# A hybrid encoder layer on one core: B parts moved behind the first block, the last pair's work laid out anew, one bank seeded

## The chip, the cores and the metric

The kernel runs on one core of a Trainium2 chip. The metric is the device time of one execution in microseconds (us). TensorE is called PE here, VectorE DVE, ScalarE ACT, GpSimd POOL and SyncE SP.

## The reference, cut to what matters

One layer is computed for 256 prompt rows and 128 sample rows (8 streams of 16), 384 rows in all, in float32, model width 2048.

```
u = rmsnorm(x);  proj = u @ w_in            # pool | z | xBC | dt | gates
A: pooling over windows 2, 4, 8, 16, a linear map per group
B: xbc = silu(causal_conv(xBC));  x, Bm, Cm = split(xbc)
   decay = exp(cum_t - cum_s) where s <= t
   y = (Cm Bm^T * decay) @ (x * dt) + (Cm @ h) * exp(cum)
   h = h * exp(last) + Bm^T (w_end * x * dt)
   y = gated_rmsnorm(y + d_skip * x, z)
m = sigmoid(g_A) * (A @ w_pool_proj) + sigmoid(g_B) * (y @ w_ssd_proj)
x = x + rmsnorm(m @ w_out)
x = x + rmsnorm(relu(rmsnorm(x) @ w_up)^2 @ w_down)
```

The outputs are the two parts of x and the new pooling, convolution and scan states.

## The kernel before, in words

Activations lie transposed in SBUF (features on the partitions, 384 rows in the free dimension). Every product with float32 weights is made of three matmuls: weight and activation are each cut into a high and a low part, and high*high, high*low and low*high are summed in one PSUM bank. For this each weight tile of 128x1024 (512 KB) is loaded by SP, cast by ACT into its high part (`wh`, line 70), and DVE subtracts to get the low part (`wl`, line 71). The three kinds of tile (`w`, `wh`, `wl`) have three buffers each, so the cast of a tile waits until PE is through with the tile three before it. A projection of 128 columns takes two such tiles, here called its halves; each is 24 matmuls (lines 101 to 103).

The scan stage runs over 8 groups of 8 heads. A group projects and convolves six column blocks (x in four, B and C), then z in four. Every group has two pairs of four heads. The work of a pair on ACT and DVE is in small functions:

- `xside`: x, turned by way of a DRAM buffer, times dt (`xdt`) and times the state's weights (`xT`), then cut into high and low (`xhl`)
- `eside(S, q)`: eight pieces of the exponent's argument (`E`) for two heads; with q = 1 the Exp over all four follows
- `dside`: the state (`hs`) times its decay; `fside(S, h2)`: half of `E` times the masked product of C and B (`cbm`)
- `bside`: B, turned, cut into high and low (`Bhl`), and two masked copies (`Bm`)

The products of a pair on PE stand in a block between two projections: `t_pp` (`pp`), `t_cb` (`cb`), `t_yT` and `t_Y` (`Y`), `t_yi` (`py`), `state` (`su`). The work of a group's second pair is spread over the next group's projections. Behind the last group there is no next one, so the last pair's work is spread over the projections of the second gate: `gate_b` calls `between` behind each half, and this takes the next piece from a list.

Every engine runs its instructions in order, and this order is decided when the program is built. `behind(ins)` puts instructions behind `ins` in that order, and `later()` puts them behind the last cast and the last subtraction of weights.

The down projection adds eight parts of 1024 features. For each part and each of four blocks of 512 columns, PE fills three PSUM banks (`wd`, one for each 128 rows `b`), and `done(b)` adds a bank to the sum in SBUF (`hacc`, line 1336). In the last part the sum is squared on ACT with the row sums in `st3` (line 1340); the last block's sum times the norm's weights goes to `z3` (line 1347); `postnorm` takes the root; line 1351 makes the four blocks of the output rows and SP stores them. In the last block all four weight tiles are held, and PE does the rows `b` = 0, 1, 2 one after the other.

## Time and profile before

| | |
|---|---|
| median of 3 runs | 2649.3 us (2647.81 to 2649.31) |
| profiled execution | 2648.75 us |
| its span, first to last instruction | 2647.0 us |
| PE busy | 2632.5 us (99%) |
| DVE busy | 1545.5 us (58%) |
| ACT busy | 1161.5 us (44%) |
| mean granted clock of TensorE | 0.999 |

A row of the timeline has the start in the span, the busy time, the engine, the line, the operation, the tiles and the count; in brackets stand the engine's idle time before it and what ended that. A row of the chain has start, length and what ran.

### The profile page before, as it was taken

To read this page: it belongs to the slowest core of one execution; us is meant where nothing else is said; L and a number is where in the kernel's file an instruction comes from. 1 tells how busy PE (TensorE), PEld (TensorE's weight loads), DVE (VectorE), ACT (ScalarE), POOL (GpSimd) and SP (SyncE) were. 2 spreads that over 40 slices of the span, in tenths; PEclk is the share of its full clock that TensorE was granted. 3 is DMA by queue.
4 is the path that set the end of the run, shared out by engine and by line. 5 is a ranking of instruction groups with operands and counts; after the bars stand their busy time and mean duration, and the time that the engine had idled before them with its cause. 6 is when DMAs were issued, how large, how long until landed. Compare 5 with 4: busy or idle time off the path is not lost.

```text
span 2647.0 us, 40715 instructions
## 1 busy us (share of the span) xinstructions
PE 2632.5 (99%) x16317; PEld 2528.3 (96%) x16317; DVE 1545.5 (58%) x2192; ACT 1161.5 (44%) x1780; POOL 242.5 (9%) x382
## 2 busy tenths in 40 slices
PE   9999999999999999999999999999999999999998
PEld 9999999999999999999999989999999999989897
DVE  6685334788888888867444436534444444444446
ACT  6443323657565656545333335433333333323233
POOL 0000002123222322311000000000000000000000
PEclk9999999999999999999999999999999999999999
DMA  7444446566666666657555543444444344444443
GB/s 275 149 133 159 148 145 207 193 200 226 215 235 197 218 228 227 221 184 257 168 162 162 188 155 134 142 137 134 137 135 137 133 137 134 136 135 137 135 137 130
DMA packets 130175, 451.50 MB, mean 171 GB/s; under 512 B 17921, under 2 KB 24641, under 8 KB 124993
## 3 DMA queue, kind: packets, MB, share of 16 engines
q1 hardware_dynamic: 103552, 361.57, 41.8%
q0 software_dynamic: 19520, 72.64, 7.7%
q10 hardware_dynamic: 6912, 14.68, 1.8%
q8 instruction: 128, 2.10, 0.3%
q14 instruction: 63, 0.51, 0.1%
HBM read 404.49 MB, written 44.34 MB: 170 GB/s over the span
## 4 chain that ended last, share of the span: by engine, by line
PE 96%; DVE 1%; DMA 1%; ACT 1%; issue 0%; POOL 0%; SPq 0%; DVEq 0%; POOLq 0%; ACTq 0%
PE pj_up L102 6%; PE pj_up L103 6%; PE pj_up L101 6%; PE wd L156 6%; PE wd L154 6%; PE wd L155 6%; PE pj_x L101 4%; PE pj_x L102 4%; PE pj_x L103 4%; PE pj_z L103 3%; PE pj_z L102 3%; PE pj_sp L102 3%; PE pj_sp L101 3%; PE pj_sp L103 3%; PE pj_z L101 3%; PE pj_ga L101 2%
## 5 line engine op out<-in xcount | busy, mean ns | idle before, releaser
L101 PE MATMUL pj_up<-x1h,wh_up 128*128 128x384 f32 (+1 forms) x1024 | 333.7, 326 | 0.0
L102 PE MATMUL pj_up<-x1l,wh_up 128*128 128x384 f32 (+1 forms) x1024 | 333.4, 326 | 0.0
L103 PE MATMUL pj_up<-x1h,wl_up 128*128 128x384 f32 (+1 forms) x1024 | 333.4, 326 | 0.0
L71 DVE TENSOR_TENSOR wl_wd<-w_wd,wh_wd 128x1024 fp32r<-128x1024 f32 x126 | 154.3, 1225 | 240.5 <-ACT wh_wd L70 240.5
L154 PE MATMUL wd<-wh_wd,hh 128*128 128x512 f32 x756 | 286.5, 379 | 0.0
L155 PE MATMUL wd<-wl_wd,hh 128*128 128x512 f32 x756 | 286.5, 379 | 0.0
L156 PE MATMUL wd<-wh_wd,hl 128*128 128x512 f32 x756 | 286.5, 379 | 0.0
L70 ACT ACTIVATE wh_wd<-w_wd 128x1024 fp32r<-128x1024 f32 x126 | 133.1, 1057 | 322.3 <-PE wd L156 261.8
L70 ACT ACTIVATE wh_up<-w_up 128x1024 fp32r<-128x1024 f32 x126 | 133.1, 1057 | 292.0 <-PE pj_up L102 231.8
L71 DVE TENSOR_TENSOR wl_up<-w_up,wh_up 128x1024 fp32r<-128x1024 f32 x126 | 154.3, 1224 | 178.1 <-ACT wh_up L70 178.0
L101 PE MATMUL pj_x<-xgh,wh_x 128*128 128x384 f32 x768 | 252.1, 328 | 0.0
L103 PE MATMUL pj_x<-xgh,wl_x 128*128 128x384 f32 x768 | 250.5, 326 | 0.1
L102 PE MATMUL pj_x<-xgl,wh_x 128*128 128x384 f32 x768 | 250.4, 326 | 0.0
L102 PEld LDWEIGHTS pj_up<-x1l,wh_up 128*128 128x128 f32 x1024 | 193.6, 189 | 0.2
L101 PEld LDWEIGHTS pj_up<-x1h,wh_up 128*128 128x128 f32 x1024 | 193.6, 189 | 0.2
L103 PEld LDWEIGHTS pj_up<-x1h,wl_up 128*128 128x128 f32 x1024 | 193.6, 189 | 0.0
L103 PE MATMUL pj_z<-xgh,wl_z 128*128 128x384 f32 x512 | 167.3, 327 | 0.0
L101 PE MATMUL pj_z<-xgh,wh_z 128*128 128x384 f32 x512 | 166.9, 326 | 0.0
L102 PE MATMUL pj_z<-xgl,wh_z 128*128 128x384 f32 x512 | 166.9, 326 | 0.0
L101 PE MATMUL pj_sp<-abh,wh_sp 128*128 128x384 f32 x512 | 166.9, 326 | 0.0
L102 PE MATMUL pj_sp<-abl,wh_sp 128*128 128x384 f32 x512 | 166.9, 326 | 0.0
L103 PE MATMUL pj_sp<-abh,wl_sp 128*128 128x384 f32 x512 | 166.9, 326 | 0.0
(330 smaller groups left out, 6180.9 us busy)
## 6 DMA issues: line engine op xcount, KB each, us to landing
w_up<-w_up SPq DMA_DIRECT2D x128, 512.0 KB, 3.5
w_wd<-w_down SPq DMA_DIRECT2D x128, 512.0 KB, 3.5
w_x<-w_in SPq DMA_DIRECT2D x96, 512.0 KB, 4.1
w_z<-w_in SPq DMA_DIRECT2D x64, 512.0 KB, 4.2
w_sp<-w_ssd SPq DMA_DIRECT2D x64, 512.0 KB, 3.5
w_ga<-w_ga SPq DMA_DIRECT2D x32, 512.0 KB, 3.5
w_pp<-w_pp SPq DMA_DIRECT2D x32, 512.0 KB, 3.5
hs<-ssm POOLq DMA_DIRECT2D x16, 1024.0 KB, 7.5
```

The costliest lines, as they stand in the source:

```text
L70: cut[0] = s.activation(h, w, AF.Copy)
L71: cut[1] = v.tensor_tensor(l, w, h.bitcast(F32), ALU.subtract)
L101: te.matmul(out, wh, xh, start=first, stop=False, **how)
L102: te.matmul(out, wh, xl, start=False, stop=False, **how)
L103: return te.matmul(out, wl, xh, start=False, stop=last, **how)
L154: te.matmul(out, mh, vh, start=k == 0, stop=False)
L155: te.matmul(out, mh, vl, start=False, stop=False)
L156: last[0] = te.matmul(out, ml, vh, start=False, stop=k == nk - 1)
```

## The change

Three places change.

First, `xside` and `eside` are cut in two (`hside` has the cut of x, `expside` the Exp), which leaves the order in the groups as it is, and in the first group `bside` is put behind the cut of the first pair's x.

```diff
             cload(D.p[1])
-            bside(D)
+            with nullcontext() if g else behind(S.split):
+                bside(D)
             dside(S)
```

On ACT in the first group stood this before (`xs1` is a block of x, `xs40` the convolved C, `wh_x3_0` the cast of a weight half):

```order
L615 ACTIVATE xs1_4391<-cacc1_4386,vec_71 128x384
L70 ACTIVATE wh_x2_1_4429<-w_x2_1_4427 128x1024
L723 ACTIVATE Bhl0_4745<-Bt0_4304 128x384
L70 ACTIVATE wh_x3_0_4476<-w_x3_0_4474 128x1024
L600 COPY cbuf0_4137<-cbuf0_4137 128x15x3
L601 COPY cstate_4135<-cbuf0_4137 128x27
L609 ACTIVATE cacc40_4464<-cbuf0_4137,vec_71 128x384
L599 COPY cbuf0_4137<-cstate_4135 128x8x3
L615 ACTIVATE xs40_4469<-cacc40_4464,vec_71 128x384
```

Now the third of these rows is gone from there, and later in the same group, on ACT, it stands here:

```order
L609 ACTIVATE cacc3_4645<-cbuf2_4141,vec_71 128x384
L779 ACTIVATE E0_0_4652<-cbc0_0_1_4307,tok_629 128x128
L723 ACTIVATE Bhl0_4745<-Bt0_4304 128x384
L788 ACT_TABLE_LOAD
L788 ACTIVATE E0_0_4652<-E0_0_4652 128x2048
L615 ACT_TABLE_LOAD
L615 ACTIVATE xs3_4650<-cacc3_4645,vec_71 128x384
```

Only this instruction moved on ACT in that group; DVE's row, POOL's and SP's are the same.

Second, the last pair's work has eight places instead of six, one behind each half of the four gates.

```diff
                 work = [
-                    lambda: xside(S),
-                    lambda: eside(S, 0),
-                    lambda: eside(S, 1),
-                    lambda: dside(S),
-                    lambda: fside(S, 0),
-                    lambda: fside(S, 1),
+                    [lambda: xside(S)],
+                    [lambda: hside(S), lambda: eside(S, 0)],
+                    [],
+                    [lambda: eside(S, 1)],
+                    [lambda: dside(S)],
+                    [lambda: expside(S)],
+                    [lambda: fside(S, 0), lambda: fside(S, 1)],
+                    [],
                 ]
```

On ACT before, from the cut of the last pair's x (`xhl7_1`) to its Exp (`wh_gb2_0` is the first half of the third gate, so the fifth half; `gbt` is a gate's sigmoid):

```order
L768 ACTIVATE xhl7_1_12254<-xT7_1_11723 128x768
L70 ACTIVATE wh_gb1_1_12259<-w_gb1_1_12257 128x1024
L777 ACTIVATE E7_1_12287<-cbc7_1_0_11888,tok_629 128x128 x8
L70 ACTIVATE wh_gb2_0_12303<-w_gb2_0_12301 128x1024
L570 ACT_TABLE_LOAD
L570 ACTIVATE gbt0_12296<-gbt0_12296 128x384
L777 ACTIVATE E7_1_12287<-cbc7_1_1_11890,tok_629 128x128 x8
L70 ACTIVATE wh_gb2_1_12342<-w_gb2_1_12340 128x1024
L785 ACT_TABLE_LOAD
L785 ACTIVATE E7_1_12287<-E7_1_12287 128x2048
L70 ACTIVATE wh_gb3_0_12378<-w_gb3_0_12376 128x1024
```

And now, over the same stretch of ACT:

```order
L70 ACTIVATE wh_gb1_1_12256<-w_gb1_1_12254 128x1024
L770 ACTIVATE xhl7_1_12284<-xT7_1_11723 128x768
L779 ACTIVATE E7_1_12287<-cbc7_1_0_11888,tok_629 128x128 x8
L70 ACTIVATE wh_gb2_0_12303<-w_gb2_0_12301 128x1024
L570 ACT_TABLE_LOAD
L570 ACTIVATE gbt0_12296<-gbt0_12296 128x384
L70 ACTIVATE wh_gb2_1_12333<-w_gb2_1_12331 128x1024
L779 ACTIVATE E7_1_12287<-cbc7_1_1_11890,tok_629 128x128 x8
L70 ACTIVATE wh_gb3_0_12376<-w_gb3_0_12374 128x1024
L570 ACTIVATE gbt1_12369<-gbt1_12369 128x384
L70 ACTIVATE wh_gb3_1_12407<-w_gb3_1_12405 128x1024
L788 ACT_TABLE_LOAD
```

The fourth half's cast (`wh_gb1_1`) moved ahead of the cut of x, the sixth's (`wh_gb2_1`) ahead of the second eight pieces of E, and the Exp moved from behind the sixth half's cast to behind the eighth's (`wh_gb3_1`). DVE's row follows: its half of the fourth weight half ahead of `xhl`, `hs` behind the seventh, and both products of E behind the ninth.

Third, in the last part and block of the down projection, bank 2 is filled with the sum so far before PE starts on it; its matmuls add to that, and `done(2)` uses the bank itself as the sum. The last product and the last store of the output are cut into two halves of 256 columns, and ACT issues the second store.

```diff
+                end = c8 == NC - 1 and nb == 3
+                held = 2 if end else None
+                if end:
+                    s.copy(o[held], hacc[:, held, blk(nb)])
...
-                    v.tensor_tensor(dst, o[b], dst, ALU.add)
+                    if b == held:
+                        dst = o[b]
+                    else:
+                        v.tensor_tensor(dst, o[b], dst, ALU.add)
...
-                        sy.dma_start(io["y"][b][:, blk(i)], z)
+                        for n, c in enumerate((slice(0, 256), slice(256, 512)) if b + i == 5 else (slice(0, 512),)):
...
+                            (s if n else sy).dma_start(io["y"][b][:, blk(i)][:, c], z[:, c])
```

In `moving`, the matmuls of the held bank have no `start`:

```diff
-            te.matmul(out, mh, vh, start=k == 0, stop=False)
+            te.matmul(out, mh, vh, start=k == 0 and b != held, stop=False, skip_group_check=b == held)
```

On DVE the end of the program was this (`wd7_3_2` is the bank, `n3_n32` the root):

```order
L1336 TENSOR_TENSOR hacc_17042<-wd7_3_2_24472,hacc_17042 128x512
L1347 TENSOR_TENSOR z3_2_24623<-hacc_17042,gpo2_17043 128x512
L1037 TENSOR_SCALAR n1_n32_24626<-st3_17046,n0_n32_24625 128x1
L1038 RECIPROCAL n3_n32_24628<-n2_n32_24627 128x1
L1039 TENSOR_SCALAR n1_n32_24626<-n1_n32_24626,n3_n32_24628 128x1
L1041 SCALAR_TENSOR_TENSOR n3_n32_24628<-n1_n32_24626,n3_n32_24628 128x1
L1351 SCALAR_TENSOR_TENSOR hacc_17042<-hacc_17042,n3_n32_24628,x1_15707 128x512 x3
L1351 SCALAR_TENSOR_TENSOR z3_2_24623<-z3_2_24623,n3_n32_24628,x1_15707 128x512
```

Now it is:

```order
L1364 TENSOR_TENSOR z3_2_24623<-wd7_3_2_24472,gpo2_17043 128x512
L1047 TENSOR_SCALAR n1_n32_24626<-st3_17046,n0_n32_24625 128x1
L1048 RECIPROCAL n3_n32_24628<-n2_n32_24627 128x1
L1049 TENSOR_SCALAR n1_n32_24626<-n1_n32_24626,n3_n32_24628 128x1
L1051 SCALAR_TENSOR_TENSOR n3_n32_24628<-n1_n32_24626,n3_n32_24628 128x1
L1369 SCALAR_TENSOR_TENSOR hacc_17042<-hacc_17042,n3_n32_24628,x1_15707 128x512 x3
L1369 SCALAR_TENSOR_TENSOR z3_2_24623<-z3_2_24623,n3_n32_24628,x1_15707 128x256 x2
```

The add is gone, `z3` reads the bank and waits for ACT's square of the same bank, and the last product stands twice at half the size. On ACT the copy into the bank stands behind the squares of the second block, and the square of the last rows (now line 1357) reads the bank.

More of the change, by code (lines that the diff above doesn't have):

```diff
@@ L143, in proj, with moving @@
         return o
-    def moving(o, units, lhs, tail, done, pool=None, own=0, hook=None, mid=None):
+    def moving(o, units, lhs, tail, done, pool=None, own=0, hook=None, mid=None, held=None):
         nk = 2 * len(units)
@@ L153, in mm @@
             out, vh, vl = pairs(o[b]), woven(wh[:, c]), woven(wl[:, c])
-            te.matmul(out, mh, vh, start=k == 0, stop=False)
-            te.matmul(out, mh, vl, start=False, stop=False)
-            last[0] = te.matmul(out, ml, vh, start=False, stop=k == nk - 1)
+            te.matmul(out, mh, vh, start=k == 0 and b != held, stop=False, skip_group_check=b == held)
+            te.matmul(out, mh, vl, start=False, stop=False, skip_group_check=b == held)
+            last[0] = te.matmul(out, ml, vh, start=False, stop=k == nk - 1, skip_group_check=b == held)
         for kp in range(n - tail):
@@ L766, in xside, with hside @@
                     )
+        def hside(S):
             S.xhl = pd.tile([P, 2, 2, 3, P], F32R, tag="xhl", name=f"xhl{S.nm}", bufs=1)
@@ L783, in eside, with expside @@
                     )
-            if q:
-                s.activation(S.E, S.E, AF.Exp, scale=-1.0)
+        def expside(S):
+            s.activation(S.E, S.E, AF.Exp, scale=-1.0)
         def fside(S, h2):
@@ L874, in build @@
                 work = [
-                    lambda: xside(S),
-                    lambda: eside(S, 0),
-                    lambda: eside(S, 1),
-                    lambda: dside(S),
-                    lambda: fside(S, 0),
-                    lambda: fside(S, 1),
+                    [lambda: xside(S)],
[6 more added lines that the diff above has]
+                    [],
                 ]
                 def between():
-                    if work:
-                        with later():
-                            work.pop(0)()
+                    with later():
+                        for fn in work.pop(0):
+                            fn()
                 for i in range(4):
@@ L907, in build @@
                 xside(prev.p[1])
+                hside(prev.p[1])
             xturned(D, g, 0)
@@ L915, in build @@
                 eside(prev.p[1], 1)
+                expside(prev.p[1])
             cload(D.p[0])
@@ L945, in build @@
                 xside(S)
+                hside(S)
             xturned(D, g, 2)
@@ L962, in build @@
                 eside(S, 1)
+                expside(S)
             cload(D.p[1])
-            bside(D)
+            with nullcontext() if g else behind(S.split):
+                bside(D)
             dside(S)
@@ L1350, in done @@
                         z = z3 if i == 3 else hacc[:, b, blk(i)]
-                        v.scalar_tensor_tensor(
-                            out=z, in0=z, scalar=y, in1=x1[:, b, blk(i)], op0=ALU.mult, op1=ALU.add
-                        )
-                        sy.dma_start(io["y"][b][:, blk(i)], z)
+                        for n, c in enumerate((slice(0, 256), slice(256, 512)) if b + i == 5 else (slice(0, 512),)):
+                            v.scalar_tensor_tensor(
+                                out=z[:, c], in0=z[:, c], scalar=y, in1=x1[:, b, blk(i)][:, c], op0=ALU.mult, op1=ALU.add
+                            )
+                            (s if n else sy).dma_start(io["y"][b][:, blk(i)][:, c], z[:, c])
                 moving(
@@ L1359, in build @@
                     hh,
-                    4 if c8 == NC - 1 and nb == 3 else 0,
+                    4 if end else 0,
                     done,
                     pg,
-                    2 if c8 == NC - 1 and nb == 3 else 0,
+                    2 if end else 0,
+                    held=held,
                 )
```

## The prediction

> **What bounds the kernel now.** I read the page first, then the waits of TensorE (PE), then the chain of work that ended last, in three stretches.

> ```profile
> span 2647.0 us, 40715 instructions
> PE 2632.5 (99%) x16317; PEld 2528.3 (96%) x16317; DVE 1545.5 (58%) x2192; ACT 1161.5 (44%) x1780; POOL 242.5 (9%) x382
> ```

> PE is busy 99% of the span, and the change leaves PE's row of instructions as it is. So only time in which PE stands still or runs slowly can be won, and the time after its last matmul. The list of PE's waits names where the first of these are (columns: total, times, longest):

> ```profile
> PE cb L666 <- ACT xs L615: 2.0, 1, 2.0
> ...
> PE pj_gb L103 <- DVE wl_gb L71: 1.0, 2, 0.7
> ```

> The first lies in the first group of the scan stage, the second between the gate projections with the last pair. These are the two places that the first two edits touch; the third edit is in the tail. I take them in turn; the sum is made against the profiled execution, 2648.75 us (span 2647.0 and 1.75 around it), which lies between the lowest run, 2647.81, and the median, 2649.3.

> **First group: the B parts go behind the block.** The chain there (start, us, what):

> ```profile
> 451.45 4.28 DMA Bt<-t_scr
> ...
> 455.75 0.02 ACT Bhl L723
> ...
> 456.18 1.06 ACT wh_x L70
> ...
> 458.40 0.62 DVE cacc L611
> ...
> 460.36 0.62 ACT xs L615
> ...
> 461.02 1.64 PE cb L666 x6
> 462.66 1.89 PE py L675 x16
> 464.55 0.56 PE pj_x L101
> ```

> ACT runs in order. Its instruction Bhl waits for the transposed B to come back from DRAM, at 455.73; queued behind it are a weight cast and the convolution of C, whose SiLU ends at 460.98, and PE's block (cb) waits for that. What ACT and DVE could do without Bhl in the row:

> ```profile
> 449.93 1.04 ACT L70 ACTIVATE wh_x<-w_x 128x1024 fp32r<-128x1024 f32 x1
> 452.15 0.61 DVE L593 TENSOR_TENSOR cbuf<-pj_x,rstd 128x192 f32<-128x192 f32 x2
> 458.68 0.33 PE L103 MATMUL pj_x<-xgh,wl_x 128*128 128x384 f32 x1
> ```

> ACT is free at 450.97 instead of 456.18. From the start of that cast to C's end the chain takes 460.98 - 456.18 = 4.80 us, which would give 455.8; DVE is at L593 until 452.76, not free at 452.0 when the cast ends, so I add 0.75: C is ready near 456.5. PE comes to the block at 458.68 + 0.33 = 459.01. The wait of 2.02 us (459.00 to 461.02) goes, with 2.5 us to spare; what is late next is PE itself.

> The wait cost more than its length. The same three pieces in the second group, and the granted clock in both places (columns of the windows: stretch, length, busy time of each engine with its count, clock, DMA share, GB/s):

> ```profile
> 548.34 0.88 PE cb L666 x6
> ...
> 551.31 0.90 PE py L675 x16
> ...
> 553.08 0.36 PE pj_x L101
> ```

> ```profile
> 462.00:464.00 2.00, 2.00 (x20) 1.02 (x18) 2.00 (x4) 2.00 (x8) 0.00 (x0) 0.50 0.01 2
> ...
> 548.00:549.30 1.30, 1.30 (x12) 1.15 (x10) 1.26 (x4) 1.28 (x4) 0.00 (x0) 1.00 0.93 189
> ```

> After the wait PE ran at half clock: 1.64 + 1.89 + 0.56 = 4.09 us against 0.88 + 0.90 + 0.36 = 2.14, so 1.95 us more. I take the slow stretch to be a consequence of the idle 2 us, since the same matmuls run at clock 1.00 elsewhere. This edit then gives 2.02 + 1.95 = 3.97 us; its bounds are 2.02 (the slow stretch stays) and 3.97. [...]

> Bhl itself, 0.52 us on ACT, now stands ahead of the Exp of the first pair, at about 472 in the new time. Followed through the same rows, ACT runs about 4.1 us earlier there than before and PE 3.97 us, so the weight cast behind the Exp keeps its place ahead of PE: nothing. Without that cover it would cost 0.5 us at most. POOL's and SP's rows do not move.

> **Last pair: the work between the gate halves.** Four gate projections (192 matmuls) run before the last block and the same number after it; here are the second and last matmul of each four:

> ```profile
> 1130.33 0.33 PE L102 MATMUL pj_gb<-xgl,wh_gb 128*128 128x384 f32 x1
> ...
> 1163.08 0.33 PE L103 MATMUL pj_gb<-xgh,wl_gb 128*128 128x384 f32 x1
> ...
> 1167.23 0.33 PE L102 MATMUL pj_gb<-xgl,wh_gb 128*128 128x384 f32 x1
> ...
> 1198.11 0.33 PE L103 MATMUL pj_gb<-xgh,wl_gb 128*128 128x384 f32 x1
> ```

> 32.75 us against 30.88: PE loses 1.87 us here, in waits for DVE's low halves of the weights. The rows behind it:

> ```profile
> 1139.34 0.56 DVE L761 TENSOR_TENSOR xT<-xT,tok 128x384 f32<-128x384 f32 x1
> ...
> 1141.68 2.43 ACT L777 ACTIVATE E<-cbc,tok 128x128 f32<-128x128 f32 x8
> ...
> 1145.09 1.23 DVE L71 TENSOR_TENSOR wl_gb<-w_gb,wh_gb 128x1024 fp32r<-128x1024 f32 x1 [1.59 <-ACT wh_gb L70]
> ...
> 1151.36 2.28 DVE L796 TENSOR_TENSOR hs<-hs,decb 128x2048 f32<-128x2048 f32 x1
> ...
> 1151.49 1.92 ACT L785 ACTIVATE E<-E 128x2048 f32<-128x2048 f32 x1
> ```

> Now the cast of the fourth half does not stand behind the split of x (xhl, which needs DVE's last xT product, to 1139.9). ACT does it while DVE still works on x, and DVE's half follows the products directly, 1139.9 to 1141.1; PE wants it at 1142.2 (the 75th matmul at 0.1625). Then in order, each step by the rows above (casts 1.05 and 1.23, eight pieces of E 2.43): the fifth half is ready at 1145.4 (wanted 1146.1), the sixth at 1148.1 (1150.0), the seventh at 1151.5 (1153.9), the eighth at 1155.0 (1157.8). No stall is left, so I take the whole 1.87 us; the bounds are 1.2 (the fifth half, with the smallest lead, 0.7 us late) and 1.87. The price is paid in E: its Exp moves behind the eighth half's cast, to about 1153 to 1155, and both products behind the ninth's, which end near 1159.6. PE wants E in the block at 1162.3, so 2.7 us of cover are left. Table loads are three as before.

> **Tail: the seeded bank.** The copy into the bank (ACT; a square of the same size takes 0.6) stands ahead of this cast, which waited 1.50 us for PE, so it costs nothing:

> ```profile
> 2611.40 1.06 ACT L70 ACTIVATE wh_wd<-w_wd 128x1024 fp32r<-128x1024 f32 x1 [1.50 <-PE wd L156]
> ```

> The end of the chain:

> ```profile
> 2638.70 0.61 DVE hacc L1336
> ...
> 2639.34 0.73 ACT q L1340 x2
> ...
> 2640.42 0.17 DVE n_n L1038
> ...
> 2643.20 0.66 DVE z L1351
> ```

> The add at 2638.70 goes and ACT squares the bank as soon as PE ends, 0.72 us earlier. But z3 now reads the same bank, and two readers of one bank are kept apart, as where the out projection's product (DVE) starts only when the square is through:

> ```profile
> 1541.30 2.13 DVE L1148 TENSOR_TENSOR hm<-wo,gpo 128x512 f32<-128x512 f32 x3 [1.00 <-ACT q L1152]
> ```

> So z3 (0.61 to 0.7 us) no longer runs beside the square: it starts when that ends, at 2639.36, and the reciprocal follows it on DVE at about 2640.1 instead of 2640.42. That is 0.3 us of the 0.72. The last product in two halves costs one more instruction, at most 0.17 (the reciprocal's row), and the last transfer is half as long and on ACT's queue. Two rows of the DMA issues (KB, us to landing), the old last store and a store of the new size from ACT:

> ```profile
> y<-z SPq DMA_DIRECT2D x1, 256.0 KB, 2.2
> ```

> ```profile
> new_ssm_p<-pe ACTq DMA_DIRECT2D x1, 128.0 KB, 1.7
> ```

> 0.5 less, minus 0.1 for the added instruction, and some of it lost since the stores ahead still fill the engines; I take 0.15. The tail gives 0.45 us, bounds -0.3 (the store on ACT's queue lands as late as 2.9) and 0.7.

> **Sum.** 3.97 + 1.87 + 0.45 = 6.29 us; 2648.75 - 6.29 = 2642.5 us, 0.24%.

> **The rivals.**

> *The slow clock stays.* If the half clock belongs to the small matmuls of the first block, or to a window that opens there anyway, only the wait goes: 2.02 + 1.87 + 0.45 = 4.34, so 2644.4 us. For it speaks that only one such stretch exists to judge by; against it, clock 1.00 at 548. [...] Chance 0.09.

> *C is still late in part, or the tail loses.* If the cast at 451 waited for its transfer by 3.5 us more, PE would stand 1 us and, without the clock falling, the gain would be 5.3: 2643.5 us; if the tail went to -0.3, 2643.2. Both near the limit of what can be told. Chance 0.12.

> *The last pair starves the block (slower).* The Exp now stands behind the cast of the eighth half in ACT's row. One weight transfer that lands late delays cast, Exp, products and block. Transfers and the longest one of the trace:

> ```profile
> w_gb<-w_gb SPq DMA_DIRECT2D x6, 512.0 KB, 3.5
> ```

> ```profile
> 425.80 10.18 DMA w_x<-w_in
> ```

> Issued near 1145.4 (when a buffer is free) and wanted at 1150.7, it has 5.3 us; with E's 2.7 us of cover it may take 8 us free of cost. Each us above that is a us of PE, and 1.95 more if the clock falls as above. The time would be that of before at 8 + 6.29 - 1.95 = 12.3 us, and with 20 us 2648.75 - 6.29 + 12 + 1.95 = 2656.4 us. Against it: three transfers in flight took 3.5, and 10.18 was measured at the start of the scan stage, among its first loads. Chance 0.04.

> **How the numbers follow.** My sum has 0.75. A measurement of this kernel can tell about 0.2%, 5.3 us, from no change: below 2644.0 is faster. The sum and half of the second rival lie there, 0.75 + 0.05, less a little for runs that differ by 1.5 us as those before did: 0.79. The clock rival and the rest of the second are within 0.2%: 0.17; the starved block is slower: 0.04. The range goes from 2641.0 (the best sum, 6.54, from the lowest run) to 2645.0 (the clock rival from the median).

> **What would show it.** PE's list of waits without cb and pj_gb; the first block's cb and py at 0.88 and 0.90 with clock 1.00; the four gates before the last block in 30.9 us; ACT's Bhl with no wait, just ahead of the Exp; z3 on DVE starting when ACT's square ends. Wrong would be a wait at cb above 0.5 us, a clock of 0.5 in the first block with no wait before it, or a wait of PE for E in the last block.

## The result, and the profile after

The changed kernel takes 2643.79 us (median; 2641.44 to 2648.55), the kernel before in the same comparison 2649.21 us (2647.26 to 2651.92). The ratio is 0.9981, 95% interval 0.9973 to 0.9988: 0.19% or 5.0 us faster by the ratio (3.2 to 7.2). The forecast was 2642.5 us, 6.29 below the profiled execution of before. The profiled execution of the changed kernel took 2643.02 us, with a span of 2641.2.

The page, and PE's list of waits, after (engine, line, what it waited for; us in total, times, longest):

```profile
span 2641.2 us, 40719 instructions
...
PE 2629.5 (100%) x16317; PEld 2527.7 (96%) x16317; DVE 1545.1 (58%) x2192; ACT 1162.2 (44%) x1781; POOL 240.9 (9%) x382
```

```profile
PE warm_o L241 <- DVE warm L237: 1.2, 1, 1.2
PE pj_x L103 <- DVE wl_x L71: 0.7, 1, 0.7
PE pj_p L103 <- DVE wl_e L303: 0.5, 1, 0.5
PE pj_gb L101 <- DVE zs L964: 0.4, 1, 0.4
```

The wait at `cb` (2.0) and the waits for `wl_gb` (1.0) are gone. There are new small ones, of pj_x and of pj_gb for zs (z of the last group); the experiments show that these come and go between executions of one order.

**First group.** The chain of waits after, and the same place in the windows (stretch, length, busy time of each engine with its count, granted clock, DMA share, GB/s):

```profile
459.28 0.88 PE cb L666 x6
460.15 1.02 PE py L675 x16
461.17 0.36 PE pj_x L101
```

```profile
459.00:461.00 2.00, 2.00 (x24) 1.39 (x22) 1.31 (x3) 1.54 (x5) 0.75 (x1) 1.00 0.35 115
461.00:463.00 2.00, 2.00 (x16) 1.90 (x13) 1.52 (x3) 1.24 (x4) 0.00 (x0) 1.00 0.96 312
```

PE goes from C's projection into the block without a gap, at clock 1.00. ACT's timeline has C's SiLU ready 2.6 us ahead of it, and Bhl where the change put it, without a wait:

```profile
456.03 0.61 ACT L615 ACTIVATE xs<-cacc,vec 128x384 f32<-128x384 f32 x1 [0.39 <-DVE cacc L611]
...
471.86 0.51 ACT L723 ACTIVATE Bhl<-Bt 128x384 fp32r<-128x384 f32 x1
```

**Last pair.** PE's timeline, the second and the last matmul of the four gate projections, and the block's reading of E; then DVE's product that makes E:

```profile
1126.64 0.33 PE L102 MATMUL pj_gb<-xgl,wh_gb 128*128 128x384 f32 x1
...
1157.51 0.33 PE L103 MATMUL pj_gb<-xgh,wl_gb 128*128 128x384 f32 x1
...
1158.65 1.94 PE L696 MATMUL Y<-E,xdt 128*32 128x256 f32 x48
```

```profile
1153.14 2.35 DVE L793 TENSOR_TENSOR E<-E,cbm 128x1024 f32<-128x1024 f32 x2
```

The four gates take 1157.51 - 1126.64 = 30.87 us (32.75 before). E is ready at 1155.49, 3.2 us ahead of its use.

**Tail.** The end of the chain, and the stores of the last block in the list of DMA issues:

```profile
2633.03 0.70 ACT q L1357 x2
...
2633.75 0.69 DVE z L1364
2634.44 0.12 DVE n_n L1047
2634.56 0.08 DVE n_n L1048
...
2635.17 0.75 DVE hacc L1369
...
2637.25 0.79 DVE z L1369 x2
```

```profile
y<-z SPq DMA_DIRECT2D x2, 256.0 KB, 2.2
y<-z SPq DMA_DIRECT2D x1, 128.0 KB, 2.2
y<-z ACTq DMA_DIRECT2D x1, 128.0 KB, 2.1
```

z3 does stand behind ACT's square. The half stores (128 KB) land in 2.1 and 2.2 us, no sooner than the whole ones (256 KB) of 2.2.

**Where the 5.7 us of span went.** I cut both traces at the same PE instructions (starts, in us; the spans end at 2646.97 and 2641.24; tk is a tile that PE fills ahead of the scan stage):

| stretch on PE | before | after | difference |
|---|---|---|---|
| span's start to the first matmul of tk | 231.40 | 230.44 | -0.96 |
| to the last matmul of C's projection, group 0 | 227.28 | 228.51 | +1.23 |
| to the second matmul behind the first block (edit A) | 6.26 | 2.42 | -3.84 |
| to the last group's second block | 660.50 | 659.94 | -0.56 |
| that block, to the second gate matmul | 4.89 | 5.33 | +0.44 |
| to the last of the four gates (edit B) | 32.75 | 30.87 | -1.88 |
| to the last matmul of the kernel | 1475.10 | 1475.10 | 0 |
| to the span's end (edit C) | 8.79 | 8.63 | -0.16 |

A, B and C are the first, second and third edit of the diff. They bring 3.84 + 1.88 + 0.16 = 5.88 us in this pair of traces; the stretches that no edit touches change by +0.15 in sum.

### The profile page after: what moved, and what is told of

The parts are those of the page before. It is cut to its first block, busy times and chain, and to the rows that moved or that the text cites. A ratio compares the mean times of both kernels' runs of the same rounds, so it can differ in the third digit from the quotient of the medians.

```text
span 2641.2 us, 40719 instructions
## 1 busy us (share of the span) xinstructions
PE 2629.5 (100%) x16317; PEld 2527.7 (96%) x16317; DVE 1545.1 (58%) x2192; ACT 1162.2 (44%) x1781; POOL 240.9 (9%) x382
## 4 chain that ended last, share of the span: by engine, by line
PE 97%; DMA 1%; DVE 1%; issue 1%; ACT 1%; SPq 0%; DVEq 0%; POOL 0%; ACTq 0%; POOLq 0%
PE pj_up L101 6%; PE pj_up L102 6%; PE pj_up L103 6%; PE wd L156 6%; PE wd L154 6%; PE wd L155 6%; PE pj_x L101 5%; PE pj_x L103 4%; PE pj_x L102 4%; PE pj_sp L103 3%; PE pj_sp L101 3%; PE pj_sp L102 3%; PE pj_z L103 3%; PE pj_z L102 3%; PE pj_z L101 3%; PE pj_gb L101 2%
## 5 line engine op out<-in xcount | busy, mean ns | idle before, releaser
L101 PE MATMUL pj_up<-x1h,wh_up 128*128 128x384 f32 (+1 forms) x1024 | 333.7, 326 | 0.0
L102 PE MATMUL pj_up<-x1l,wh_up 128*128 128x384 f32 (+1 forms) x1024 | 333.4, 326 | 0.0
L103 PE MATMUL pj_up<-x1h,wl_up 128*128 128x384 f32 (+1 forms) x1024 | 333.4, 326 | 0.0
L71 DVE TENSOR_TENSOR wl_wd<-w_wd,wh_wd 128x1024 fp32r<-128x1024 f32 x126 | 154.3, 1225 | 240.3 <-ACT wh_wd L70 240.3
L156 PE MATMUL wd<-wh_wd,hl 128*128 128x512 f32 x756 | 286.5, 379 | 0.0
L70 ACT ACTIVATE wh_wd<-w_wd 128x1024 fp32r<-128x1024 f32 x126 | 133.1, 1057 | 321.6 <-PE wd L156 261.2
L70 ACT ACTIVATE wh_up<-w_up 128x1024 fp32r<-128x1024 f32 x126 | 133.1, 1057 | 292.0 <-PE pj_up L102 231.8
L71 DVE TENSOR_TENSOR wl_up<-w_up,wh_up 128x1024 fp32r<-128x1024 f32 x126 | 154.3, 1225 | 178.0 <-ACT wh_up L70 178.0
L101 PE MATMUL pj_x<-xgh,wh_x 128*128 128x384 f32 x768 | 252.0, 328 | 0.3 <-ACT wh_x L70 0.3
L103 PE MATMUL pj_x<-xgh,wl_x 128*128 128x384 f32 x768 | 250.5, 326 | 0.7 <-DVE wl_x L71 0.7
L102 PE MATMUL pj_x<-xgl,wh_x 128*128 128x384 f32 x768 | 250.4, 326 | 0.0
L102 PEld LDWEIGHTS pj_up<-x1l,wh_up 128*128 128x128 f32 x1024 | 193.6, 189 | 0.2
L101 PEld LDWEIGHTS pj_up<-x1h,wh_up 128*128 128x128 f32 x1024 | 193.6, 189 | 0.2
L103 PEld LDWEIGHTS pj_up<-x1h,wl_up 128*128 128x128 f32 x1024 | 193.6, 189 | 0.0
L103 PE MATMUL pj_z<-xgh,wl_z 128*128 128x384 f32 x512 | 167.2, 327 | 0.0
L101 PE MATMUL pj_z<-xgh,wh_z 128*128 128x384 f32 x512 | 166.9, 326 | 0.0
L102 PE MATMUL pj_z<-xgl,wh_z 128*128 128x384 f32 x512 | 166.9, 326 | 0.0
L101 PE MATMUL pj_sp<-abh,wh_sp 128*128 128x384 f32 x512 | 166.9, 326 | 0.0
L102 PE MATMUL pj_sp<-abl,wh_sp 128*128 128x384 f32 x512 | 166.9, 326 | 0.0
L103 PE MATMUL pj_sp<-abh,wl_sp 128*128 128x384 f32 x512 | 166.9, 326 | 0.0
## 6 DMA issues: line engine op xcount, KB each, us to landing
w_up<-w_up SPq DMA_DIRECT2D x128, 512.0 KB, 3.5
w_wd<-w_down SPq DMA_DIRECT2D x128, 512.0 KB, 3.5
w_x<-w_in SPq DMA_DIRECT2D x96, 512.0 KB, 4.0
w_z<-w_in SPq DMA_DIRECT2D x64, 512.0 KB, 4.4
w_sp<-w_ssd SPq DMA_DIRECT2D x64, 512.0 KB, 3.5
w_ga<-w_ga SPq DMA_DIRECT2D x32, 512.0 KB, 3.5
w_pp<-w_pp SPq DMA_DIRECT2D x32, 512.0 KB, 3.5
```

The costliest lines, as they stand in the source:

```text
L70: cut[0] = s.activation(h, w, AF.Copy)
L71: cut[1] = v.tensor_tensor(l, w, h.bitcast(F32), ALU.subtract)
L101: te.matmul(out, wh, xh, start=first, stop=False, **how)
L102: te.matmul(out, wh, xl, start=False, stop=False, **how)
L103: return te.matmul(out, wl, xh, start=False, stop=last, **how)
L156: last[0] = te.matmul(out, ml, vh, start=False, stop=k == nk - 1, skip_group_check=b == held)
```

## The experiments

Each run is read by the same stretches, since its time scatters by some us. Ratios are against the kernel before, on the same chip. The kernels with repeats and the two orders of the last pair's work were executed once each.

**One edit at a time.** The kernel before, with the lines of the diff for `bside` alone; for the last pair's `work` (with `hside` and `expside`) alone; for `held`, the seed and the two halves alone.

> The kernel before with the first edit alone (the B parts of the first group behind the split of x). Theory (half clock follows the wait): PE has no wait at cb, cb takes 0.88 and py 0.90 us at clock 1.00, and from the last matmul of C's projection to the second matmul behind the block it takes about 2.4 us where it took 6.3: 3.97 us less, about 0.15%. Rival (the slow clock belongs to this place): the wait of 2.02 us goes, cb and py stay at 1.64 and 1.89, 2.0 us less. Second question: the new wait of 0.4 us of PE for DVE's zs at the first gate projection; if it comes from this edit, it shows here.

> The kernel before with the second edit alone (the last pair's work laid out anew). Theory: the four gate projections ahead of the last block take 30.9 us from their second matmul to their last, where they took 32.75; 1.87 us less, about 0.07%, under what the times can tell. The half clock in the first group stays as before (cb 1.64). If the new wait for zs belongs to this edit, it shows here at 0.4 us and leaves 1.45 of the 1.87.

> The kernel before with the third edit alone (seeded bank, last product and store in halves). From the start of the last matmul to the end of the span it took 8.82 us before and 8.59 with all three edits; here the same 8.6 if the tail stands by itself. My forecast said 8.37 (0.45 less). The times cannot tell it: within 0.02%.

| kernel | median, us | ratio, 95% | C's projection to behind the block | gates | tail |
|---|---|---|---|---|---|
| A alone | 2645.78 | 0.9987, 0.9979 to 0.9996 | 2.42 | 32.75 | 8.79 |
| B alone | 2648.21 | 0.9996, 0.9987 to 1.0004 | 5.20 | 30.88 | 8.79 |
| C alone | 2650.48 | 1.0003, 0.9995 to 1.0012 | 7.67 | 31.50 | 8.62 |

The edits act apart: A and B shorten their own stretch and leave the others as they are, and C its tail; what differs beside that in C alone (7.67 and 31.50) is taken up below. Only A alone can be told from no change by its times. The wait for zs (0.3) shows in A alone and not in B alone. Of the eleven traces with edit A five have it above 0.3 us and none of the three without: it needs neither B nor C, and whether A has a part in it stays open.

The first group without edit A came out differently in each execution. The transfer of B in the chain of waits and the block in PE's timeline, first of B alone:

```profile
451.92 3.85 DMA Bt<-t_scr
```

```profile
461.06 1.14 PE L666 MATMUL cb<-xs,xs 128*128 128x256 f32 x6 [1.80 <-ACT xs L615]
462.13 1.09 PE L675 MATMUL py<-hs,Cm 128*32 128x256 f32 x16
463.89 0.40 PE L101 MATMUL pj_x<-xgh,wh_x 128*128 128x384 f32 x1 [0.67 <-DVE cbuf L593]
```

Then of C alone, the same two views:

```profile
451.16 5.72 DMA Bt<-t_scr
```

```profile
462.17 1.43 PE L666 MATMUL cb<-xs,xs 128*128 128x256 f32 x6 [3.61 <-ACT xs L615]
463.53 1.96 PE L675 MATMUL py<-hs,Cm 128*32 128x256 f32 x16
```

The wait follows the transfer that brings B back: 3.85, 4.28 and 5.72 us of transfer, 1.80, 2.02 and 3.61 us of wait. And behind 1.80 us the clock did not fall at all (1.00 from 461 to 465, py 1.09), though 2.02 us had brought half clock (0.50). I had expected 1.64 for cb in B alone; it took 1.14. So the half clock is not simply the price of the wait, and this had to be settled.

The last row of B alone shows something else. At full clock PE came through the block early and stood again, 0.67 us, for DVE's cbuf. DVE was as late in the kernel before; first its row there, then the same one of B alone:

```profile
463.09 0.61 DVE L593 TENSOR_TENSOR cbuf<-pj_x,rstd 128x192 f32<-128x192 f32 x2
```

```profile
463.12 0.62 DVE L593 TENSOR_TENSOR cbuf<-pj_x,rstd 128x192 f32<-128x192 f32 x2
```

So a good part of the slow clock in before fell into time in which PE would have waited for DVE in any case. The stretch took 6.26 us there and 5.20 in B alone; less the 0.22 us by which its wait at cb was longer, the half clock made the difference of 0.84 us, in this one pair of traces, and not of 1.95.

**A wait made to measure.** The changed kernel, where ACT writes the first tap of C's convolution several times; the count differs by run and group (c is 40 in group 0; line numbers behind it are one or two higher):

```diff
-            s.activation(seg(a), b[:, :, 0:16], AF.Copy, scale=w(0))
+            for _ in range(7 if c == 40 else 1):
+                s.activation(seg(a), b[:, :, 0:16], AF.Copy, scale=w(0))
```

> The changed kernel; in the first group ACT repeats the first tap of C's convolution (the same result written again) 6 times more, about 0.52 us each. C's SiLU, ready 2.6 us ahead of PE, comes about 3.1 us later, so PE waits about 0.5 us at cb. Theory (the clock falls behind a wait of about 2 us): clock 1.00, cb 0.9, py 0.9. Rival (any wait at this place brings the slow stretch): cb near 1.6 and py near 1.9.

> The same with 8 repeats: C about 4.2 us later, a wait of about 1.6 us at cb. If the clock falls at a length of idle time between 0.5 and 2.0 us, this places it: half clock behind 1.6 (cb 1.6, py 1.9, 3.6 us lost in all) or none (cb 0.9, 1.6 us lost).

> The same with 10 repeats: C about 5.2 us later, a wait of about 2.6 us, longer than the 2.02 of the kernel before, and with the B parts where the change put them. Theory (the wait brings the half clock): clock 0.50 over about 3.4 us behind the wait, cb 1.6, py 1.9, so 2.6 + 1.95 = 4.6 us lost. Rival (the B parts or the small matmuls brought it before): clock 1.00 and 2.6 us lost.

> The changed kernel; the repeats, 9, stand in the second group instead, where the trace of before shows clock 1.00. C's SiLU there is 2.4 us ahead of cb and comes about 4.7 us later, so PE waits about 2.3 us ahead of cb. Theory (the half clock follows the wait, wherever it is): cb, Y, py and su behind it run at 0.50 for about 3.4 us, and some 1.7 us are lost beside the wait. Rival (it belongs to the first group): clock 1.00 and only the wait is lost.

The waits came out longer than expected, 2.08, 3.54, 5.88 and 4.79 us, since a repeat costs 0.65 and not 0.52 us of ACT and a weight cast slips in between. All four were followed by half clock (0.50), in the second group as in the first, with the B parts where the change put them. So the B parts and the place have no part in it. But the slow stretch lasted 3.4 us in the first of the four and 6.8 in the others. The windows of the kernel with 8 repeats:

```profile
460.54:463.94 3.40, 0.87 (x6) 0.57 (x4) 2.10 (x5) 2.70 (x5) 0.76 (x1) 1.00 0.51 161
463.95:467.35 3.40, 2.40 (x10) 1.82 (x14) 2.32 (x5) 3.07 (x11) 0.00 (x0) 0.50 0.40 119
467.36:470.76 3.40, 3.40 (x22) 2.36 (x15) 2.67 (x6) 0.65 (x3) 0.00 (x0) 0.50 0.57 211
470.77:474.10 3.33, 3.33 (x22) 3.33 (x21) 2.42 (x6) 1.85 (x4) 1.43 (x3) 1.00 0.07 16
```

The slow clock begins inside the wait (PE stands from 461.41 to 464.95; 0.50 from 463.94) and ends 6.83 us later, in the midst of matmuls. Each trace has a second slow start, in the tail, when PE is done. I read both starts from narrow windows, to some 0.05 us, and took the distance:

| kernel | first start | tail | distance | in steps of 3.4133 |
|---|---|---|---|---|
| before | 461.51 | 2642.62 | 2181.11 | 639.0 |
| C alone | 462.88 | 2640.58 | 2177.70 | 638.0 |
| 6 repeats | 461.60 | 2639.30 | 2177.70 | 638.0 |
| 8 repeats | 463.94 | 2648.48 | 2184.54 | 640.0 |
| 10 repeats | 463.28 | 2647.81 | 2184.53 | 640.0 |
| 9 repeats, second group | 546.35 | 2645.55 | 2099.20 | 615.0 |

All distances are whole steps of 3.4133 us. The step can be read from the last run of this group, with waits in all eight groups: between 462.20 and 1124.39 its clock changed 14 times, each time whole steps from the first, and 662.19 / 194 = 3.4133. So in these traces the clock changes on a grid, which lies differently to the program from one execution to the next: a border 0.90 us ahead of the wait at cb in before, and 0.93 us behind its start in B alone. With it the case of B alone is read: its tail start is 2641.30, 639 steps back is 460.19, and this border cuts the wait (459.26 to 461.06) into 0.93 and 0.87 us; with 0.38 of the wait for cbuf the second stretch holds 1.25 us of idle time. In before, the whole 2.02 lies in the stretch from 458.10 to 461.51. The last run put this to the test, with waits in all eight groups:

> The changed kernel with repeats of the first tap of C's convolution in all eight groups: 5 in groups 0, 1, 3, 5 and 7, 6 in groups 2, 4 and 6, so that PE waits ahead of cb about 1.4 to 1.6 us in the first five and about 2.1 to 2.3 in the other three. Theory from the runs so far: the clock is granted over stretches of 3.413 us on a grid that runs free of the program; a stretch follows at 0.50 when PE stood idle for 2.0 us or more in the one before (the starts at 461.5, 462.9, 461.6 and so on lie whole numbers of 3.413 us from the slow start in the tail of the same run), and not at 1.25 or less. So the five short waits bring no half clock unless the limit lies below 1.6; of the three longer ones those bring it that lie within one stretch of the grid, known from the tail, and those that a border cuts do not. Rival (the length of the wait alone decides, at some 2 us): all three longer waits are followed by half clock, wherever the grid lies.

The waits were longer than expected again (1.89 to 4.24 us). Its windows, cut at the grid as counted back from its tail (slow from 2680.86): the second group's place, where a border cuts the wait, then the fourth's, where none does, and what follows that:

```profile
547.53:550.94 3.41, 1.91 (x14) 1.72 (x12) 2.96 (x5) 1.08 (x3) 0.00 (x0) 1.00 0.40 89
550.95:554.36 3.41, 2.69 (x44) 2.12 (x48) 2.74 (x7) 2.76 (x6) 0.00 (x0) 1.00 0.32 130
735.27:738.68 3.41, 1.52 (x11) 1.28 (x10) 3.00 (x7) 1.48 (x3) 0.00 (x0) 1.00 0.70 210
738.68:742.09 3.41, 3.41 (x35) 2.35 (x37) 1.94 (x3) 1.49 (x5) 0.00 (x0) 0.50 0.25 34
742.10:745.51 3.41, 3.41 (x69) 2.68 (x62) 3.41 (x7) 2.50 (x8) 0.95 (x1) 1.00 0.32 125
```

And the two waits in its timeline of PE:

```profile
551.67 1.14 PE L668 MATMUL cb<-xs,xs 128*128 128x256 f32 x6 [2.24 <-ACT xs L617]
...
738.08 1.53 PE L668 MATMUL cb<-xs,xs 128*128 128x256 f32 x6 [1.89 <-ACT xs L617]
```

The longer wait, 2.24 us, was followed by clock 1.00, the shorter, 1.89 us, by 0.50: length alone does not decide, and the rival falls. In the stretch of the grid the idle time was 3.41 - 1.91 = 1.50 us in the one and 3.41 - 1.52 = 1.89 in the other. The other six waits put 2.0 to 2.9 us into one stretch and all were followed by half clock, starting on the grid. So in these traces the limit lies between 1.50 and 1.89 us of idle time in a stretch of 3.41. The expectation that waits of 1.4 to 1.6 us stay free could not be tried, since none came out so short.

The tails narrow it, since PE's work ends inside a stretch there. In C alone and with 6 repeats 2.13 and 2.04 us of that stretch were idle, and the next ran at 0.50. In B alone it was 1.66, and the next still ran at 1.00. The nearest is `exp_late`, one of the two orders of the last pair's work below; its last matmul's stretch and the next:

```profile
2634.79:2638.20 3.41, 1.54 (x8) 1.01 (x6) 2.76 (x7) 0.98 (x3) 0.00 (x0) 1.00 0.80 308
2638.21:2641.61 3.40, 0.00 (x0) 0.00 (x0) 3.10 (x7) 0.00 (x0) 0.00 (x0) 1.00 0.44 169
```

Here 3.41 - 1.54 = 1.87 us idle left the clock at 1.00. By this count the limit lies near 1.9 us; as the ends of matmuls are modelled in the profile, 1.87 and 1.89 can't be told apart.

**The last pair, taken apart.** Two orders of `work` in the changed kernel; the first (`half_first`) keeps only the later place of `hside`, the second (`exp_late`) puts only that back:

```diff
 # half_first
+    [xside], [hside, eside 0], [eside 1, expside], [dside], [fside 0], [fside 1], [], []
 # exp_late
+    [xside, hside], [eside 0], [], [eside 1], [dside], [expside], [fside 0, fside 1], []
```

> The changed kernel, with the last pair's work in the order of before but for one thing: the split of x (xhl) goes to the second place, behind the cast of the fourth half of the gate weights. Theory: a part of the 1.87 us was the fourth half behind xhl; what the Exp ahead of the sixth half's cast and DVE's product with hs ahead of a low half cost stays. From the second to the last matmul of the four gates 31.2 to 32.3 us. Rival (all of it was the fourth half): 30.9.

> The complement: the changed kernel with the split of x back in the first place, ahead of the fourth half's cast; E pieces, Exp and products where the change put them. Theory: the fourth half comes 0.9 us late at PE (DVE's half after ACT's wait, 1143.1 against 1142.2 in the times of before), the rest is in time: 31.4 to 31.9 us. Rival (the Exp was all of it): 30.9.

The gates took 31.72 and 31.86 us. One row of PE's timeline of each, with what it waited for:

```profile
1145.75 0.43 PE L103 MATMUL pj_gb<-xgh,wl_gb 128*128 128x384 f32 x1 [0.29 <-DVE wl_gb L71]
```

```profile
1141.74 0.43 PE L103 MATMUL pj_gb<-xgh,wl_gb 128*128 128x384 f32 x1 [0.67 <-DVE wl_gb L71]
```

With the later split of x alone the fourth half is in time and 31.72 - 30.87 = 0.85 us stay lost behind the Exp and hs, first at the sixth half (the first row). With all but that, the fourth half is late again (the second row) and 0.99 stay lost. The two parts of the edit add up, 0.99 + 0.85 = 1.84 of 1.88, and neither is the whole: both rivals fall.

**The tail.** All three edits, once with the last product and store whole, and once also with z3 behind the second sum:

```diff
-  for n, c in enumerate((slice(0, 256), slice(256, 512)) if b + i == 5 else (slice(0, 512),)):
+  for n, c in enumerate((slice(0, 512),)):
```

> All three edits, but the last product and store of the last block in one piece again. My forecast: the split brings 0.15 us, so from the last matmul's start to the end 8.59 + 0.15 = 8.74. Rival, from the trace of the changed kernel: the second half's store lands in 2.1 us, no sooner than a whole one, and the added instruction costs 0.1 to 0.2, so the tail without the split is 8.40 to 8.45, 0.15 to 0.2 shorter.

> All three edits without the split of the last store, and the product of the seeded bank (z3, 0.69 us on DVE) moved behind the second of the last block's four sums, ahead of the last two. DVE's chain of small instructions for the norm then starts when ACT's square ends, 0.69 us earlier, and the first two stores leave 0.69 us earlier; z3 takes its 0.69 later, so the last product ends at the same time unless DVE stood idle for the root meanwhile. If the end is set by the data engines (four stores of 256 KB that fill them), the tail is up to 0.6 us shorter than without the split: 7.8 to 8.0 us from the last matmul's start. Rival (the end is set by DVE's last product and its store): no change, 8.4.

| kernel | median, us | ratio, 95% | tail |
|---|---|---|---|
| without the split | 2643.86 | 0.9977, 0.9968 to 0.9986 | 8.41 |
| and z3 later | 2642.91 | 0.9973, 0.9962 to 0.9984 | 8.40 |

The end of the chain without the split:

```profile
2641.55 0.66 DVE z L1369
```

The last product ends at 2642.21, and the span 3.11 us later, at 2645.32; with the split it ended at 2638.04, and the span 3.20 us later, at 2641.24. The split costs 8.63 - 8.41 = 0.22 us and brings nothing: 0.13 by DVE's added instruction (0.79 for two halves against 0.66), 0.09 behind it. In the second kernel z3 did not go where I wrote it: in its row on DVE it came behind the first small instruction of the norm, into the time in which DVE waits for ACT's root. The timeline of DVE there:

```profile
2633.76 0.21 DVE L1047 TENSOR_SCALAR n_n<-st,n_n 128x1 f32<-128x1 f32 x1 [0.61 <-ACT q L1357]
2633.89 0.68 DVE L1369 TENSOR_TENSOR z<-wd,gpo 128x512 f32<-128x512 f32 x1
2634.49 0.15 DVE L1048 RECIPROCAL n_n<-n_n 128x1 f32<-128x1 f32 x1
```

By the timelines the reciprocal starts 1.87 us behind the last matmul's start, as with z3 in front (2634.49 - 2632.62 here, 2638.78 - 2636.91 without the split). Stores that leave 0.69 us earlier were so not tried, and this run decides nothing between its theory and its rival. By the tails both kernels without the split are 0.2 us better than the changed one; the times can't tell these apart.

## Why the prediction was right, and where it was not

- **The wait at cb.** Right in every step: C ready at 456.64 (forecast 456.5), 2.6 us ahead of PE (forecast 2.5), PE at the block without a wait, cb 0.88. The block's py took 1.02 where I took the second group's 0.90, hence 3.84 for 3.97.
- **The half clock behind it.** The 1.95 us are gone, as said, but two things in this step were too simple. One is "a consequence of the idle 2 us". In these traces the half clock followed 1.89 us or more of idle time in a grid stretch of 3.41 us and not 1.87 or less, and whether a wait does that hangs on where the grid lies in that execution (2.24 us, cut by a border, did not; 1.89 us in one stretch did). An estimate from these numbers, with every position of the grid taken as equally likely: a wait of 2.02 us lies whole in one stretch in (3.41 - 2.02) / 3.41 = 0.41 of all positions; with the cut ones whose longer part still exceeds a limit of 1.87 to 1.89, it is about half. The other is the price. 1.95 us is the time that the slow matmuls took more, but without the slow clock PE would have waited for DVE's cbuf in much of it: B alone lost 5.20 - 2.42 = 2.78 us at full clock, with a wait at cb of 1.80. So of the 3.84 us that edit A brought, about 0.84 hung on the clock and 3.0 on the late Bhl, where the forecast had 1.95 and 2.02. The sum came out because edit A takes away both.
- **A draw.** The wait itself differed too: 1.80, 2.02 and 3.61 us in three executions, so the stretch took 5.20, 6.26 and 7.67 us against 2.42. Edit A brought 2.78, 3.84 or 5.25 us against these; the times of A alone say 3.4 (1.1 to 5.6). That the one trace read for the forecast lay in the middle of the three was luck.
- **The rival of the slow clock that stays** fell: in A alone the block ran at full clock (the stretch 2.42 us), and with repeats the half clock (0.50) came in the second group too.
- **Bhl ahead of the Exp.** It cost nothing, as forecast: no wait on it, and from the first block's py to the next one PE takes 42.86 or 42.87 us in all seven traces with the edit and an undisturbed first group. One thing stays open. The stretch from there to the last group took 660.5 to 660.8 us in the three traces without the edit and 659.9 to 662.4 in the six with the edit and no repeats, by low halves of the z weights that come late by some 0.3 to 0.4 us each. The edit changes no order in those groups, and three against six traces do not tell whether it has a part in this. If it has, by the means of these traces, it is some 0.7 us of what the edit brings.
- **The last pair.** 1.87 forecast, 1.88 found, with E ready 3.2 us ahead (forecast 2.7). The order of waits was read rightly: 1.0 us from the fourth half behind xhl, the rest from the Exp and hs ahead of later halves. Here too before is a draw: in C alone the fourth half came in time by itself and the gates took 31.50.
- **The tail.** This term was mis-sized. The bank filled with the sum brought 8.79 - 8.41 = 0.38 us (forecast 0.3, from the reciprocal 0.3 earlier; by the chain it is 0.29 earlier, 1.95 us behind the last matmul's start where it was 2.24, and the last products start 0.38 earlier). The split, forecast at +0.15, cost 0.22: I had priced the half store by a lone one of 128 KB (1.7 us) and it landed in 2.1, behind three whole stores. The tail gave 0.16 for 0.45.
- **The starved block** (the rival on the slower side) did not come: E was 3.2 us early.

The edits' sum in the traces, 5.88, is 0.41 under the forecast of 6.29: 0.13 from the first group and 0.29 from the tail, with 0.01 of B the other way. The times' 5.0 (3.2 to 7.2) hold both. What else moves between executions is larger than this rest: the way from tk to C's projection took 226.96 to 229.68 us over all traces.

## What to carry to other kernels

A wait that the profile shows once is a draw: look at the transfer that sets it (B's took 3.85 to 5.72 us here, the wait 1.80 to 3.61), and where a step hangs on a DRAM round trip, take it out of an in-order queue ahead of work that PE needs. Price a lost clock by its chance as well as its size, and only by the part in which no other engine would have held PE up anyway (here about 0.84 of 1.95 us). A store split in two, behind full stores, brought nothing here and cost one more instruction (0.22 us in the tail).

## What the runs showed of the hardware

```profile
926.41:929.82 3.41, 2.46 (x12) 1.96 (x13) 2.74 (x6) 2.75 (x6) 0.00 (x0) 0.50 0.33 130
929.82:933.23 3.41, 3.41 (x52) 2.35 (x52) 1.78 (x4) 0.00 (x0) 0.00 (x0) 0.50 0.50 154
```

- The last stores, behind three of 256 KB, landed in 2.1 to 2.2 us at 128 KB and at 256 KB alike.
